# All query, key and value projections ahead of the stick-breaking attention, ten of the twelve tiles in pairs by seven block products

## Chip, cores and metric

The kernel runs on one core of a Trainium2 chip. The metric is the device time of one launch in microseconds, the median of several runs. A core has TensorE (PE: matmuls, with its weight loads shown apart as PEld), VectorE (DVE), ScalarE (ACT), GpSimd (POOL) and SyncE (SP, which only issues transfers); each works through its own instructions in order.

## What is computed

One layer of an encoder on a prompt of 1024 rows and a sample of 32 rows with a past of 512. The parts that matter here:

```python
p = h @ w_in                      # h: 1056 x 1024; columns: 384 q-latent | 256 kv-latent | 32 rope |
                                  #    512 SB q | 512 SB k | 512 SB v | 1024 gate A | 1024 gate B
def sb_attend(q, qpos, k, v, kpos):            # 8 heads of 64, strictly causal, no softmax
    z = einsum('bqhd,bshd->bhqs', q, k) * 64 ** -0.5
    sp = where(mask, softplus(z), 0.0)
    later = cumsum(sp, axis=3, reverse=True) - sp
    a = where(mask, exp(log_sigmoid(z) - later), 0.0)
    return einsum('bhqs,bshd->bqhd', a, v)
merged = sigmoid(gate A) * (o_A @ w_proj_a) + sigmoid(gate B) * (o_B @ w_proj_b)
```

`o_B` is this attention, `o_A` a latent attention with softmax that runs after it. The new keys and values are outputs too. Then come an output projection, a residual, and a convolutional feed-forward net (up-projection, down-projection). Everything is float32.

## The kernel before

**Precision.** Each operand of a product is split in a high part (rounded by ScalarE, `hi`) and a low part (the rest, by VectorE, `lo`). A product is three matmuls, high x high, high x low, low x high, added in PSUM (`mm3`, `prod`). So a *direct tile* of 128 output columns is 3 column blocks of 352 x 8 steps of the contraction x 3 = 72 matmuls (`mtile`), with the 1024 x 128 weights as the loaded operand and the transposed `h` (`Hht`, `Hlt`: 128 partitions x 8 x 1056) streaming.

**Block products.** The up-projection further down computes two such tiles together: weights and `h` are seen as 2 x 2 blocks (two halves of the contraction, two halves of the 1056 columns on the one side; the two tiles on the other), and seven products of sums of blocks take the place of eight. Each product is `prod` on column blocks of 256 and 272. Weight sums are made per pair of tiles, the sums of `h` blocks once.

**Stages, in order.** `stage_h` norms, transposes and splits `h`. `stage_sb` goes over four pairs of heads (`sb_pair`). For a pair it projects the query, key and value tile directly, splits them, turns keys and values to the row layout with TensorE transposes (`to_natural`) for the outputs and the value operand, and runs the attention of the two heads (`sb_attend`). The order of TensorE, ScalarE and VectorE within the attention is written out by hand in `ORDER`: `S` score matmuls, `a e l x c d E` the steps of the weights, `T h v` the transposed weights and their split, `V` the value product, `o p` its eviction. Among them stand `f` (three matmuls of a gate tile, or four small matmuls of a modulation product, `ada_step`), `G` (a gate block's eviction and store) and `W`/`w` (high and low part of the next gate tile's weights), which keep TensorE supplied: four of the sixteen gate tiles for each pair. The sample's rows get an attention of their own (`sb_sample`, in two halves after the second and fourth pair); its second part, `sample_rest`, runs under the next projections. `stage_lat` then makes five latent tiles directly (two kv, three q), their norms and the rotary keys, and `stage_mla` the second attention.

Outside the hand-ordered parts a planner of the tile framework orders the instructions of each engine by priority (program order) and its own cost estimates. A tile is a named buffer; a new tile of the same name and number of buffers waits until the old one is no longer read. Raw weights go through two buffers `wr`, loaded by SyncE; the splits go to two buffers each of `wh` and `wl`. Stores go through GpSimd.

Of the kernel before, what the change touches and what calls it, by code (L numbers as in the profile page):

```python
# [8 lines left out]
F32 = mybir.dt.float32  # L9
# [8 lines left out]
P = 128  # L18
# [26 lines left out]
class K:  # L45
# [9 lines left out]
    BUFS = {"A": 5, "Q": 3, "big": 3, "o": 2, "QZ": 1, "t": 5, "mh": 4, "ml": 4, "dh": 3, "dl": 3, "ada": 1, "G": 1, "Gs": 1, "xs": 1, "jk": 1, "s": 3, "pv": 1, "tr": 2, "mm": 2, "KSm": 1, "VSm": 1, "ObH": 1, "ObL": 1}  # L55
# [106 lines left out]
    def late_vectors(self):  # L162

        nc, a = self.nc, self.a
        v = self.tl(self.At, [P, TP], F32, "A")
# [109 lines left out]
    def norm_T(self, t0, xs, g, sv, tp, k0=0, k1=KT):  # L275
# [3 lines left out]
        if t0 < 8:  # L279
# [3 lines left out]
            for k in range(k0, k1, m):  # L283
                tr = self.bank("tr")
                f = self.tl(tp, [P, 512], F32, "hf").rearrange("p (k c) -> p k c", k=m)
# [15 lines left out]
        else:  # L301
# [3 lines left out]
            f = self.tl(tp, [P, 512], F32, "hf")[:, :256].rearrange("p (k t) -> p k t", t=TS)  # L305
# [98 lines left out]
    def to_natural(self, f, outs, ev):  # L404

        nc = self.nc
        for t0 in (0, 4, 8):
            tr = self.bank("tr")
            n = 4 if t0 < 8 else 1
            for j in range(n):  # L410
                r = P if t0 < 8 else TS
                nc.tensor.transpose(tr[:r, j * P : j * P + P], f[:, (t0 + j) * P : (t0 + j) * P + r], self.idt)
            ev(tr, t0, n, P if t0 < 8 else TS)

    def sb_pair(self, p):
        nc, a = self.nc, self.a
        q0, k0, v0 = 672 + p * P, 672 + 512 + p * P, 672 + 1024 + p * P

        Qe = self.tl(self.Sp, [P, TP], F32R, "Q")
        Qo = self.tl(self.Sp, [P, TP], F32R, "Q")  # L420
        wh, wl = self.w_in_tile(q0)
        for c0, n, ps in self.mtile(wh, wl, self.Hh, self.Hl, self.BLK, KT):
            m = min(n, TP - c0)
            c = slice(c0, c0 + m)
            self.hi(Qe[0:64, c], ps[0:64, :m], 0.125)
            self.hi(Qo[64:128, c], ps[64:128, :m], 0.125)
            st = nc.vector.scalar_tensor_tensor
            st(Qe[64:128, c], ps[0:64, :m], 0.125, Qe[0:64, c].bitcast(F32), ALU.mult, ALU.subtract)
            st(Qo[0:64, c], ps[64:128, :m], 0.125, Qo[64:128, c].bitcast(F32), ALU.mult, ALU.subtract)
            if m < n:  # L430
                nc.scalar.mul(self.qsb[:, p], ps[:, m:n], 0.125)
        if p == 2:
            self.sample_rest()

        KHe = self.tl(self.Sp, [P, TP], F32R, "KH")
        KHo = self.tl(self.Sp, [P, TP], F32R, "KH")
        KLe, KLo = self.KLz
        kf = self.tl(self.At, [P, BIG], F32, "big")
        wh, wl = self.w_in_tile(k0)
        for c0, n, ps in self.mtile(wh, wl, self.Hh, self.Hl, self.BLK, KT, "mm" if p else "s"):  # L440
            nc.scalar.copy(kf[:, c0 : c0 + n], ps[:, :n])
        s = slice(0, TP)
        nc.vector.tensor_copy(KHe[0:64, s], kf[0:64, s])
        nc.vector.tensor_copy(KHo[64:128, s], kf[64:128, s])
        self.lo(KLe[0:64, s], kf[0:64, s], KHe[0:64, s])
        self.lo(KLo[64:128, s], kf[64:128, s], KHo[64:128, s])
        self.hi(KHe[64:128, s], kf[0:64, s])
        self.hi(KHo[0:64, s], kf[64:128, s])
        nc.gpsimd.tensor_copy(self.ksb[:, p], kf[:, TP:T])

        def ev_out(name, after=None):
            def ev(tr, t0, n, r):
                st = self.tl(self.Sp, [P, n * P], F32, "nat" if n > 1 else "nat1")
                nc.scalar.copy(st[:r, : n * P], tr[:r, : n * P])
                pc = slice(2 * p, 2 * p + 2)
                if t0 < 8:
                    dst = a[f"sb{name}_p"][0, 0, t0 * P : (t0 + n) * P, pc].rearrange("(j r) h d -> r j (h d)", r=P)
                else:
                    dst = a[f"sb{name}_s"][0, 0, :, pc].rearrange("r h d -> r (h d)").unsqueeze(1)
                nc.gpsimd.dma_start(dst, st[:r, : n * P].rearrange("r (j c) -> r j c", j=n))  # L460
                if after:
                    after(st, tr, t0, n, r)
            return ev

        self.to_natural(kf, None, ev_out("k"))

        V = self.tl(self.Sp, [P, 8, 2, P], F32R, "V")
        vf = self.tl(self.At, [P, BIG], F32, "big")
        wh, wl = self.w_in_tile(v0)
        for c0, n, ps in self.mtile(wh, wl, self.Hh, self.Hl, self.BLK, KT):  # L470
            nc.scalar.copy(vf[:, c0 : c0 + n], ps[:, :n])

        def vsplit(st, tr, t0, n, r):
            if t0 < 8:
                sv = st.rearrange("r (j h d) -> r j h d", j=4, h=2)
                nc.vector.tensor_copy(V[:, t0 : t0 + 4, :, 0:64], sv)
                nc.vector.tensor_tensor(V[:, t0 : t0 + 4, :, 64:128], sv,
                                        V[:, t0 : t0 + 4, :, 0:64].bitcast(F32), ALU.subtract)
            else:
                nc.gpsimd.tensor_copy(self.vsb[:, p * P : p * P + P], st[:r, :P])  # L480

        self.to_natural(vf, None, ev_out("v", vsplit))

        def score(h, ps, i, c0, n):
            q = slice(i * P, (i + 1) * P)
            Q, KH, KL = (Qe, KHe, KLe) if h == 0 else (Qo, KHo, KLo)
            nc.tensor.matmul(ps[:, :n], Q[:, q], KH[:, c0 : c0 + n], start=True, stop=False)
            nc.tensor.matmul(ps[:, :n], Q[:, q], KL[:, c0 : c0 + n], start=False, stop=True)


        self.in_w.append(self.w_in_tile(2208 + 4 * p * P))
        if p == 0:
            self.late_vectors()
        E = mybir.EngineType
        with self.tc.manual_schedule(engines={E.PE, E.Activation, E.DVE}):
            self.sb_attend(score, V, self.store(self.obd[p]), self.gates(range(4 * p, 4 * p + 4)))
        if p % 2:
            self.sample_rest = self.sb_sample(p // 2)

# [24 lines left out]
        v7.0 f1 V7.1 f2 V7.0 f1 o7 f1 p7 f2 G f7 G  # L524
    """.split()

    def sb_attend(self, score, V, out, fill):
# [3 lines left out]
        common = self.sums(V, out, tiles)  # L531
        for x in self.ORDER:
            k, x = x[0], x[1:]
# [89 lines left out]
    def values(self, h, u, jb, pv, V, pt):  # L623
        for s in range(2):
            b = 2 * jb + 1 - s
            for j, x in enumerate(pt):
                self.nc.tensor.matmul(pv[:, :256], V[:, b, h], x[:, s * 256 : s * 256 + 256],
                                      start=(jb == u and s == 0 and j == 0), stop=(jb == 0 and s == 1 and j == 1))
# [1725 lines left out]
```

## Time and profile before

| | |
|---|---|
| runs | 1705.4, 1707.41, 1704.56 us; median 1705.4 |
| profiled execution | 1709.09 us; span 1707.3 us; granted clock 0.994 |
| four attention pairs, first score to last value product | 84.3 to 158.5, 200.5 to 274.0, 322.6 to 396.1, 438.0 to 511.6 us |
| latent stage | about 520 to 611 us |

The span is the time from the first to the last instruction. Busy times are shares of it; a matmul's duration overlaps the next one's, so the pace of TensorE is read from what follows it. Lnnn is a line of the kernel.

### The profile page before, as it was taken

How to read it: one execution, taken by the hardware profiler on the slowest of the kernel's cores; microseconds unless marked ns; L12 is line 12 of the kernel's file. 1: busy time of each engine (PE TensorE's matmuls, PEld its weight loads, DVE VectorE, ACT ScalarE, POOL GpSimd, SP SyncE). 2: the span in 40 equal slices, each digit the busy share in tenths (PEclk: the TensorE clock that was granted, in tenths of full speed). 3: DMA queues.
4: the chain of work that ended last, by engine and by line, in shares of the span. 5: the costliest groups of instructions: out<-in, count | busy, mean ns of one | idle time of the engine just before them, and what ended most of it. 6: DMA issues, size and time to landing. Idle time of an engine off the chain costs nothing. (4 is left out here: it accounts for less than half of the span.)

```text
span 1707.3 us, 29721 instructions
## 1 busy us (share of the span) xinstructions
PE 1674.0 (98%) x11526; PEld 1525.1 (89%) x11526; DVE 1235.1 (72%) x2065; ACT 978.2 (57%) x1902; POOL 276.6 (16%) x530
## 2 busy tenths in 40 slices
PE   5999999999999999999999999999999999999998
PEld 3899999999999898988889789999999999977886
DVE  4597495593782488787776779887787787788456
ACT  4496595593783477777773476544444444545442
POOL 2211111111110121110100121211121121110013
PEclk8999999999999999999999999999999999999999
DMA  9234343233442331222174531423333333697653
GB/s 330 82 115 126 93 125 96 87 108 86 135 130 58 98 84 55 68 76 67 63 269 148 175 125 61 143 94 130 130 100 131 131 102 131 228 328 249 227 151 121
DMA packets 169805, 224.33 MB, mean 131 GB/s; under 512 B 13326, under 2 KB 115872, under 8 KB 169664
## 3 DMA queue, kind: packets, MB, share of 16 engines
q1 hardware_dynamic: 153216, 177.11, 32.9%
q0 software_dynamic: 16224, 45.24, 7.6%
q8 instruction: 90, 1.47, 0.4%
q14 instruction: 51, 0.42, 0.1%
q10 hardware_dynamic: 224, 0.09, 0.0%
HBM read 170.34 MB, written 51.25 MB: 130 GB/s over the span
## 5 line engine op out<-in xcount | busy, mean ns | idle before, releaser
L65 ACT ACTIVATE wh<-wr 128x1024 fp32r<-128x1024 f32 (+5 forms) x153 | 130.7, 861 | 257.9 <-PE s L1808 79.6
L68 DVE TENSOR_TENSOR wl<-wr,wh 128x1024 fp32r<-128x1024 f32 (+5 forms) x153 | 150.3, 988 | 139.3 <-ACT wh L65 139.1
L72 PE MATMUL mm<-hh,wh 128*128 128x352 f32 x688 | 230.4, 335 | 0.0
L73 PE MATMUL mm<-hl,wh 128*128 128x352 f32 x688 | 224.4, 326 | 0.0
L74 PE MATMUL mm<-hh,wl 128*128 128x352 f32 x688 | 223.3, 325 | 0.0
L72 PEld LDWEIGHTS mm<-hh,wh 128*128 128x128 f32 x688 | 130.2, 189 | 7.7 <-issue 3.1
L73 PEld LDWEIGHTS mm<-hl,wh 128*128 128x128 f32 x688 | 130.2, 189 | 2.8 <-DVE hl L300 1.2
L74 PEld LDWEIGHTS mm<-hh,wl 128*128 128x128 f32 x688 | 130.0, 189 | 0.4 <-issue 0.4
L1809 PE MATMUL s<-T,wl 128*128 128x256 f32 (+1 forms) x328 | 93.6, 285 | 0.0
L1808 PE MATMUL s<-T,wh 128*128 128x256 f32 (+1 forms) x328 | 93.4, 285 | 0.0
L1807 PE MATMUL s<-T,wh 128*128 128x256 f32 (+1 forms) x328 | 93.3, 284 | 0.0
L1948 DVE SCALAR_TENSOR_TENSOR u<-u,c,u 128x1058 f32<-128x1058 f32 x68 | 87.0, 1316 | 1.9 <-ACT u L1945 0.7
L613 PE MATMUL tr<-c,A 128*128 128x128 f32 x576 | 84.5, 274 | 0.6 <-DVE A L729 0.3
L1807 PE MATMUL tr<-T,wh 128*128 128x272 f32 (+1 forms) x272 | 77.8, 286 | 0.0
L1809 PE MATMUL tr<-T,wl 128*128 128x272 f32 (+1 forms) x272 | 77.6, 285 | 0.2 <-DVE wl L68 0.2
L1808 PE MATMUL tr<-T,wh 128*128 128x272 f32 (+1 forms) x272 | 77.3, 284 | 0.0
L68 DVE TENSOR_TENSOR wl<-S,wh 128x1024 fp32r<-128x1024 f32 x40 | 48.9, 1223 | 36.8 <-ACT wh L65 36.8
L613 PEld LDWEIGHTS tr<-c,A 128*128 128x128 f32 x576 | 67.1, 141 | 7.8 <-ACT A L552 1.6
L1809 PE MATMUL mm<-T,wl 128*128 128x256 f32 (+1 forms) x256 | 73.0, 286 | 0.3 <-DVE wl L68 0.2
L1807 PE MATMUL mm<-T,wh 128*128 128x256 f32 (+1 forms) x256 | 73.0, 285 | 0.0
L1808 PE MATMUL mm<-T,wh 128*128 128x272 f32 (+1 forms) x256 | 72.7, 284 | 0.0
L68 DVE TENSOR_TENSOR PTl<-tr,PTh 128x512 fp32r<-128x512 f32 x96 | 64.5, 683 | 7.1 <-ACT PTh L65 6.8
(694 smaller groups left out, 5441.6 us busy)
## 6 DMA issues: line engine op xcount, KB each, us to landing
wr<-in_w_ada_dram SPq DMA_DIRECT2D x48, 512.0 KB, 4.5
wr<-in_w_up_dram SPq DMA_DIRECT2D x44, 512.0 KB, 3.9
dr<-in_w_down_dram SPq DMA_DIRECT2D x43, 512.0 KB, 5.0
wr<-in_w_in_dram SPq DMA_DIRECT2D x33, 512.0 KB, 4.9
wr<-gdn SPq DMA_DIRECT2D x30, 512.0 KB, 4.4
gdn<-u POOLq DMA_DIRECT2D x23, 512.0 KB, 5.4
gd<-nat POOLq DMA_DIRECT2D x48, 176.0 KB, 2.2
t<-gd SPq DMA_DIRECT2D x16, 528.0 KB, 6.1
```

Source lines behind the costliest of these rows:

```text
L65: self.nc.scalar.activation(out, in_, AF.Identity, scale=scale)
L68: return self.nc.vector.tensor_tensor(out, full, hi.bitcast(F32), ALU.subtract)
L72: m(ps, lh, rh, start=start, stop=False)
L73: m(ps, lh, rl, start=False, stop=False)
L74: self.pe = m(ps, ll, rh, start=False, stop=stop).ins
L613: self.nc.tensor.transpose(tr[:, (2 * s + q) * P : (2 * s + q + 1) * P], at[q][:, b * P : b * P + P], self.idt)
L1807: m(ps[:, :n], w[0][:, k], x[0][:, k, c], start=first and k == 0, stop=False, skip_group_check=True)
L1808: m(ps[:, :n], w[0][:, k], x[1][:, k, c], start=False, stop=False, skip_group_check=True)
L1809: i = m(ps[:, :n], w[1][:, k], x[0][:, k, c], start=False, stop=k == 3, skip_group_check=True)
L1948: nc.vector.scalar_tensor_tensor(y, u[:, w : w + YW], self.cvT[:, w, cc : cc + 1], y, ALU.mult, ALU.add)
```

## The change

All twelve query, key and value tiles are made ahead of the attention, in a new `stage_qkv`. The query and key tile of the first pair of heads are direct, and so is one q-latent tile (taken out of `stage_lat`, kept in DRAM). The other ten go in five pairs through seven block products, as in the up-projection. `stage_h` keeps the float32 `h` of the second half of the rows (`fq`), from which the sums `T1` to `T4` of `h` blocks are made while the direct tiles run. Finished high and low parts of queries and keys, and the values in row layout, are stored to DRAM (`spill`, `vd`) through GpSimd.

The attention then runs for the four pairs without projections between. The operands of a head are loaded by SyncE into single buffers: those of the next pair's first head behind the last score (`S3.1b`) and the last value product (`V3.0`) of the first head, those of the second head behind `S7.1b` and `V7.0`. The gate tiles run on through all four pairs; the first weight split of the next pair moves into the end of `ORDER`. Both halves of the sample's attention move to the latent stage, with the sample's operands kept in DRAM. The rotary table `qt` and the diagonal buffers are set up later; zeroing goes from VectorE to GpSimd.

The diff's core:

```diff
     def stage_h(self):
+        self.Fq = self.tc.alloc_tile_pool(name="fq", bufs=1, reuse_waits="tile")
+        self.fq = self.Fq.tile([P, KT, TP - 512 + TS], F32, name="fq")
...
+    def stage_qkv(self):
+        T4, T3, T1, T2 = ([Tp.tile([P, 4, HC], F32R, name=self.nm("T")) for _ in range(2)] for _ in range(4))
+        B11, B21, B22 = quad(0, 0), quad(4, 0), quad(4, 1)
+        F12, F22 = (self.fq[:, k : k + 4, 16:] for k in (0, 4))
...
+        def half(x):
+            if cnt["half"] % 2 == 0:
+                self.hs = [self.tl(self.W, [P, 1024], F32R, g) for g in ("wh", "wl")]
...
+        def sums():
+            c2 = slice(0, 264), slice(264, HC)
+            for i, q in enumerate((Q1, Q2, Q3, Q1)):
+                c, x = slice(132 * i, 132 * i + 132), q.rearrange("p (k c) -> p k c", k=4)
+                add(x, F22[:, :, c], F12[:, :, c], ALU.subtract)
+                self.hi(T3[0][:, :, c], x)
+                self.lo(T3[1][:, :, c], x, T3[0][:, :, c])
+            for c in c2:
+                x = F12[:, :, c]
+                add(x, x, fl(B11[0][:, :, c]), ALU.subtract)
+                add(x, x, fl(B11[1][:, :, c]), ALU.subtract)
+            for c in c2:
+                add(F22[:, :, c], F22[:, :, c], F12[:, :, c], ALU.subtract)
+            hi(T2, F22)
+            lo(T2, F22)
+            yield
+            hi(T1, F12)
+            lo(T1, F12)
+            yield
+            for c in c2:
+                x = F22[:, :, c]
+                add(x, fl(B21[0][:, :, c]), x, ALU.subtract)
+                add(x, x, fl(B21[1][:, :, c]), ALU.add)
+            hi(T4, F22)
+            lo(T4, F22)
+            yield
+        def pair(i, ta, tb, ua, ub):
+            ra, rb = raws.pop(0)
+            a0, a1 = half(ra[:, :512]), half(ra[:, 512:])
+            X, Y = ([self.bank(g) for _ in range(2)] for g in ("mm", "s"))
+            for ps, w, x in ((X, a0, B11), (Y, a1, B21)):
+                for b in range(2):
+                    prod(ps[b], b, w, x, True)
...
+            for b in range(2):
+                prod(X[b], b, w1, T2, False)
+                nc.scalar.copy(Q2[:, cs[b]], X[b][:, : ns[b]])
...             # then w2 x T1, w3 x T3, w4 x T4, w5 x B22 in the same way
+        pairs = ((("v", 0), ("v", 1)), (("k", 1), ("q", 1)), (("k", 2), ("k", 3)), (("v", 2), ("v", 3)), (("q", 2), ("q", 3)))
...
     ORDER = """ ...
-        v7.0 f1 V7.1 f2 V7.0 f1 o7 f1 p7 f2 G f7 G
+        v7.0 f1 V7.1 f2 V7.0 f1 o7 f1 W p7 f2 w G f7 G
...
     def stage_sb(self):
+        def queries(p, h):
+            r, o = slice(64 * h, 64 * h + 64), slice(64 - 64 * h, 128 - 64 * h)
+            d = lambda x, n: nc.sync.dma_start(x.bitcast(F32), self.spilt[n][p][r])
+            if p:
+                Q[h], KH[h] = t(f"Q{h}"), t(f"KH{h}")
+            d(Q[h][r], "qh")
+            d(KH[h][r], "kh")
+            d(KH[h][o], "kh")
+            d(Q[h][o], "ql")
+            d(self.KLz[h][r], "kl")
...
-        for p in range(4):
-            self.sb_pair(p)
+        fill = self.gates()
+        for p in range(4):
+            then = {} if p == 3 else {"S3.1b": lambda: queries(p + 1, 0), "V3.0": lambda: values(p + 1, 0),
+                                      "S7.1b": lambda: queries(p + 1, 1), "V7.0": lambda: values(p + 1, 1)}
+            with self.tc.manual_schedule(engines={E.PE, E.Activation, E.DVE}):
+                self.sb_attend(score, lambda b, h: V[h][:, b * P : b * P + P], self.store(self.obd[p]), fill, then)
...
     def stage_lat(self):
         self.sample_rest()
+        rest = self.sb_sample(0)
         fc += latent(4, 1, lp, "lt")
+        rest()
...
-        for m in range(3):
+        nc.sync.dma_start(x2, self.l2d)
+        for m in (2, 0, 1):             # m = 2 is read from DRAM, 0 and 1 are projected
```

More of the change, by code (lines that the diff above doesn't have):

```diff
@@ L445, in sb_pair @@
[L445 to L498, printed above, removed]
+            self.hi(QH[:, c], ps[:, :m], 0.125)
+            stt(QL[:, c], ps[:, :m], 0.125, fl(QH[:, c]), ALU.mult, ALU.subtract)
+            if m < n:
+                nc.scalar.mul(self.qsb[:, 0], ps[:, m:n], 0.125)
```

313 lines of the change are left out of this document (239 added, 74 removed).

## The prediction

> **What bounds the kernel now.** I read the page's first part, then the busy time by stretches (columns: us, then PE, PEld, DVE, ACT and POOL busy with their counts, granted clock, DMA share, GB/s). The stretches are the three projections between two pairs of heads (164.9 to 200.4), the attention of the first pair (84.3 to 164.9), a stretch of the later up-projection, which already makes seven block products for eight (1156.8 to 1402.5), and the latent stage (520 to 611).
>
> ```profile
> span 1707.3 us, 29721 instructions
> PE 1674.0 (98%) x11526; PEld 1525.1 (89%) x11526; DVE 1235.1 (72%) x2065; ACT 978.2 (57%) x1902; POOL 276.6 (16%) x530
> 164.90:200.40 35.50, 35.49 (x226) 34.90 (x225) 10.81 (x15) 11.28 (x22) 3.60 (x5) 1.00 0.29 80
> 84.30:164.90 80.60, 80.54 (x573) 74.93 (x572) 69.38 (x124) 65.24 (x144) 14.85 (x27) 1.00 0.41 119
> 1156.80:1402.50 245.70, 245.70 (x2049) 242.99 (x2050) 192.80 (x290) 117.08 (x189) 46.49 (x117) 1.00 0.36 119
> 520.00:611.00 91.00, 90.14 (x669) 83.77 (x667) 43.62 (x85) 39.99 (x86) 14.75 (x26) 1.00 0.31 87
> ```
>
> TensorE is never free in any of them, at full clock. Between pairs VectorE and ScalarE are busy only 10.8 and 11.3 of 35.5 us, so there the time is the matmuls' alone; in the attention they follow at 69 and 65 of 80.6 us. A saved matmul column in a projection is saved time, as long as nothing else becomes late.
>
> A busy TensorE is not a pace, because matmuls overlap. The pace comes from the evictions on ScalarE, which waits for the matmuls (ACT in order of time: start, duration; in brackets the idle time before and who ended it). First two blocks of one value tile, then the same eviction of two successive up-projection channels.
>
> ```profile
> 195.81 0.45 ACT L471 COPY big<-mm 128x352 f32<-128x352 f32 x1 [3.33 <-PE mm L74]
> 199.65 0.45 ACT L471 COPY big<-mm 128x352 f32<-128x352 f32 x1 [3.38 <-PE mm L74]
> ...
> 1158.36 0.37 ACT L1920 COPY q<-mm 128x256 f32<-128x256 f32 x1 [2.12 <-PE mm L1809]
> 1178.83 0.37 ACT L1920 COPY q<-tr 128x256 f32<-128x256 f32 x1 [0.43 <-PE tr L1809]
> ```
>
> A block is 8 x 3 = 24 matmuls of 352 columns: 3.84 us, 0.160 each. A tile of three blocks is 11.52, two tiles are 23.04 us. A channel is two tiles by seven products: 7 x 2 column blocks x 4 x 3 = 168 matmuls of 256 or 272 columns in 20.47 us, 0.122 each.
>
> **The change part by part.** *The products.* Five pairs of tiles go from 144 matmuls to 168 narrower ones, by the same helper and widths as the up-projection. 5 x (23.04 - 20.47) = **-12.9 us**. Of 17 direct tiles before (12 here, 5 in the latent stage), two query/key tiles and the latent tile stay direct in the new stage and four in the latent stage. The 72 turns of keys and values, the 16 gate tiles and the modulation products stay. So the rest of the sum is what is no longer hidden.
>
> *Does the pair of tiles keep TensorE's pace?* The work per pair, by rows that group instructions (count, busy us, mean ns of one, idle before): three on VectorE in the up-projection, then one each on VectorE, ScalarE and GpSimd between two pairs of heads.
>
> ```profile
> L68 DVE TENSOR_TENSOR wl<-S,wh 128x1024 fp32r<-128x1024 f32 x24 | 29.4, 1224 | 25.8 <-ACT wh L65 25.8
> L1899 DVE TENSOR_TENSOR S<-wr 128x512 f32<-128x512 f32 x12 | 8.3, 691 | 16.7 <-DMA wr<-in_w_up_dram 16.7
> L1884 DVE TENSOR_TENSOR u<-s,q 128x256 f32<-128x256 f32 (+1 forms) x105 | 32.5, 334 | 3.9 <-PE s L1809 2.1 <-ACT q L1920 1.8
> ...
> L428 DVE SCALAR_TENSOR_TENSOR Q<-mm,Q 64x352 fp32r<-64x352 f32 x2 | 1.0, 518 | 5.4 <-ACT Q L65 5.4
> L65 ACT ACTIVATE wh<-wr 128x1024 fp32r<-128x1024 f32 x2 | 2.1, 1060 | 6.0 <-PE mm L73 6.0
> L875 POOL DMA_DIRECT2D gd<-nat x1 | 0.5, 547 | 4.1 <-ACT nat L874 4.1
> ```
>
> Seven half splits (7 x 0.69), four weight sums (4 x 0.69), six additions of 0.33 make 9.6 us, the splits of finished tiles 2 to 5 more: at most 15 of 20.5. In the up-projection VectorE is busy 193 of 246 us, 78%, and the pace holds. I take 0.
>
> *The block sums, once.* Four operand sums over 4 x 528 = 2112 columns need six additions and four low parts: 21,120 columns. At 1224 ns for 1024 that is 25.2 us of VectorE. They can start when the last normed block is there (the last low part of the normed input on VectorE, then the first score on TensorE, as it is today):
>
> ```profile
> 61.29 0.22 DVE L68 TENSOR_TENSOR hl<-hf,hh 128x128 fp32r<-128x128 f32 x1
> 84.30 0.36 PE L487 MATMUL s<-KH,Q 128*128 128x256 f32 x1
> ```
>
> The three direct tiles now there end just before 84.3, less the value tile's turns: about 83. With the two first products, 2 x 20.47/7 = 5.8 us, the second sum is needed at 88.9, the first at 91.8, and the last (two products on) at 97.6. VectorE to the second sum: six of the ten parts, 15.1 us, plus 1.6 of query low parts (three of 0.52) and 1.2 of weight split: ready at 61.5 + 17.9 = 79.4. Then 4.2 for the pair's first weights, 1.2 for a key's low part, 2.5 for the first sum: 87.3. Then 4.3 of weights and additions, and 3.8 for the first half of the last sum: 95.4 against 97.6. It just fits if nothing waits. From 0 (it fits) to 6.5 (each low part first waits for its high part on ScalarE: 8448 columns at 1060 ns for 1024 are 8.7 us, less 2.2 of room); I take **+1.5**, near the end the count gives.
>
> *First scores.* The new stage's operand buffers become the attention's tiles. The first head's five half-height loads (256 KB each) can be issued when the third-last product is done, so two products, 5.8 us, cover them. Rows (DMA issues in the first pair's attention, KB each, us to landing; then the issue time of one on SyncE, min/median/max ns; then a stretch in which DMA was full):
>
> ```profile
> wr<-in_w_ada_dram SPq DMA_DIRECT2D x6, 512.0 KB, 4.6
> out_dram<-nat POOLq DMA_DIRECT2D x2, 256.0 KB, 3.5
> ob<-o POOLq DMA_DIRECT2D x8, 64.0 KB, 3.2
> L210 SPq DMA_DIRECT2D wr<-in_w_ada_dram x32: 327/340/1759, 69.3 to 489.8; - x32
> 20.00:40.00 20.00, 14.98 (x73) 9.86 (x67) 12.15 (x21) 13.04 (x21) 5.14 (x8) 0.59 1.04 369
> ```
>
> Five issues of 0.34 and a landing of 3.5 make 5.2 us; 1.31 MB at 369 GB/s is 3.6 us, on top of a latency of some 3. So from 0 to 11.7 (five landings one after another, 17.5 less 5.8); I take **+1.5**, by the overlapping rows. The Trainium skill, "SBUF — State Buffer", section "Door 1: The DMA port swizzle", says that 64 neighbouring partitions reach only 8 of the 16 ports. By it those loads run at half rate, 1.31 MB in 7.1 us, and this term would be about 5 us; no row here shows a 64-partition load on SyncE, and the case is a rival below.
>
> *Between pairs.* The projections between pairs also hid the attention's tail. ScalarE at the end of the first pair, the first scores after the projections (PE), and the same tail's weight split in the second pair:
>
> ```profile
> 158.54 0.36 ACT L599 COPY o<-pv 64x256 f32<-64x256 f32 x1 [2.29 <-PE pv L627]
> 164.64 0.43 ACT L874 COPY nat<-mm 128x352 f32<-128x352 f32 x1
> ...
> 200.46 0.36 PE L487 MATMUL s<-KH,Q 128*128 128x256 f32 x1
> 201.31 0.34 PE L488 MATMUL s<-KLz,Q 128*128 128x384 f32 x1
> ...
> 267.95 1.06 ACT L65 ACTIVATE wh<-wr 128x1024 fp32r<-128x1024 f32 x1 [0.93 <-DMA wr<-in_w_in_dram]
> ```
>
> The tail is filled with gate matmuls until about 163.8. Now the next pair's scores follow (0.9 us), then the modulation product, whose second weight can only be fetched into the buffer that the new `W`/`w` split frees: o7 at 158.5, high part 1.06, low part 1.22, some 161.3, plus issue and landing (0.34 + 4.6) 166.2, against 165.3 needed. That is 0.8 at each of three boundaries: **+2.4** (0 to 3 x 3). Head reloads have the whole other head's time, some 40 us (half of 80.6); they cost nothing unless SyncE holds something back (rival below). The other new transfers (16 spills of queries and keys, 8 of values, one latent tile, through GpSimd) add 25 x 0.55 us to an engine busy 3.6 of 35.5; I take 0.
>
> *Latent stage.* It loses one tile (11.5 us) of cover and gains the first half of the sample's attention, whose matmuls come along from the projections of the third pair. Today's stalls there:
>
> ```profile
> 296.05 0.66 PE L785 MATMUL pv<-A,big 128*128 128x64 f32 x4 [0.33 <-ACT A L772]
> 553.82 0.63 PE L1030 MATMUL tr<-c,nat 128*128 128x128 f32 x4 [0.82 <-DMA nat<-in_cache_mla_krope_dram]
> ```
>
> Two stalls of 0.3 and 0.8 us. The sample's first half gets the second latent tile as its new cover, VectorE and ScalarE are half idle (44 and 40 of 91). From -0.3 to +4; I take **+1.0**, net of the first stall **+0.7**. The rotary table, loaded later, has the key and value products before its first use: 0.
>
> Sum: -12.9 + 1.5 + 1.5 + 2.4 + 0.7 = **-6.8 us**. The profiled execution took 1709.1 us, its span 1707.3; the median of the runs is 1705.4. Taken off each: 1702.3 for the profiled execution, **1698.6** for the median.
>
> **The rivals.**
> *All cover holds* (products gain in full, every other term at its lower end): -12.9 - 0.3 = -13.2, 1692.2. For it: the up-projection's pace without a stall. Chance 0.25.
>
> *The first pair and the first scores come late*: sums at some 6 us and half-rate loads at 5 instead of 1.5 each: -6.8 + 8 = +1.2, 1706.6. For it: VectorE just fits, ScalarE and VectorE hand the sums to each other, and 64 KB from 64 partitions took 3.2 us where 256 KB from 128 took 3.5. Against: the loads use both halves in turn. Chance 0.14.
>
> *SyncE's one queue starves the gates* (the slower case). The head reloads wait on SyncE for the last score of the old head, and the weight loads of the gate tiles stand behind them. Today SyncE waits long for buffers (waits by who released: us in total, times, longest):
>
> ```profile
> SPq L82 <- PE mm L212: 150.8, 16, 13.6
> ```
>
> and the tail's split above waited 0.93 us for its weights, so these have no slack. ScalarE and TensorE run in a written order and would stop behind the late split. At 2.5 us for each of six places (two heads, three boundaries) it is +15: -6.8 + 15 = +8.2, 1713.6. It turns the result from 1.1 us a place. Against: the loads are placed just after those scores, where little else is due. Chance 0.13.
>
> *It does not do what it says*: if a matmul cost its weight load and not its columns, 24 more a pair at 0.160 would add 3.84 instead of taking 2.57: +19.2 - 6.8 + 12.9 = +25, 1731. The row against it: the weight loads are busy 98 to 99% in both stretches, yet the pace follows the columns (0.160 for 352, 0.122 for 264 on average). The Trainium skill, "Perfetto Trace Analysis", section "Identifying the Most-Contended Engine", judges TensorE's headroom by that busy share; the trace shows the share equal and the pace different, so I leave it 0.02.
>
> **How the numbers follow.** The forecast has 0.46. What a measurement of this kernel can tell from no change is 0.2%, 3.4 us. Faster: the forecast, full cover and a part of the late case (0.03): 0.74. Same: most of the late case: 0.11. Slower: SyncE's queue and weight loads: 0.15. The range 1691.0 to 1706.6 holds forecast, full cover and late case: 0.85, and their edges leave some 0.8.
>
> **What would show it.** Right: 120 more matmuls; the five pairs at 20.5 us each; the first scores at 83 + 5 x 20.47 and the turns of keys and values, 186 to 196 us; pair periods of 80 to 82 us instead of 116; the latent stage shorter by a tile. Wrong: gaps on TensorE released by VectorE's sums, by loads of queries or keys, or by ScalarE waiting for gate weights at the boundaries; a pace over 0.125 us in the block products; attention periods well over 82 us.

## The result, and the profile after

The changed kernel is slower: 1729.5 us (1728.6 to 1731.7) against 1705.0 us for the kernel before on the same chip, a ratio of 1.0143 (95%: 1.0126 to 1.0161). The forecast was 1698.6, the range 1691.0 to 1706.6. The profiled execution took 1731.7 us.

Page, first part, and busy time by stretches of the changed kernel (us, then PE, PEld, DVE, ACT, POOL busy with counts, granted clock, DMA share, GB/s): two steady stretches of the seven products, then the first block pair (80 to 110), then the first scores (200 to 230).

```profile
span 1729.9 us, 30270 instructions
PE 1669.2 (96%) x11646; PEld 1518.2 (88%) x11646; DVE 1273.2 (74%) x2129; ACT 992.7 (57%) x1934; POOL 294.6 (17%) x566
160.00:180.00 20.00, 20.00 (x169) 19.98 (x168) 8.74 (x14) 9.66 (x19) 4.71 (x8) 1.00 0.56 172
180.00:200.00 20.00, 20.00 (x169) 19.96 (x168) 11.66 (x21) 8.18 (x20) 5.30 (x9) 1.00 0.48 151
80.00:90.00 10.00, 8.36 (x66) 7.91 (x64) 5.90 (x7) 3.68 (x8) 3.17 (x5) 1.00 0.47 162
90.00:100.00 10.00, 2.82 (x10) 2.33 (x11) 10.00 (x12) 6.01 (x7) 0.00 (x0) 0.52 0.00 0
100.00:110.00 10.00, 9.94 (x66) 9.66 (x66) 7.89 (x12) 2.91 (x6) 0.00 (x0) 0.79 0.42 105
200.00:210.00 10.00, 8.54 (x71) 8.30 (x69) 5.45 (x11) 3.48 (x8) 5.46 (x11) 1.00 1.08 308
210.00:220.00 10.00, 1.54 (x13) 0.81 (x13) 2.72 (x3) 2.11 (x2) 3.84 (x8) 0.67 1.04 361
220.00:230.00 10.00, 5.78 (x23) 4.51 (x23) 1.81 (x5) 2.98 (x9) 0.19 (x1) 0.65 0.85 317
```

There are 120 more matmuls and 5 us less TensorE time (1669.2 against 1674.0). In the steady stretches 169 matmuls take 20 us, one more than a pair's 168 in the forecast 20.5. The loss stands in two places of some 20 us each, where TensorE is nearly empty.

I added up, over the trace, each matmul's distance to the next one beyond its pace in a steady stretch (0.160 us for 352 columns, 0.122 for 264, and so on). From 30 us to the first score of the later, latent attention this idle time is 33.2 us more than before, the work at pace is 13.2 us less: 20.0 us longer in all. The rest of the kernel adds 2.5 us at its end, which no run here explains.

**First place: the first block pair.** TensorE in order of time (idle time before, and who ended it); then VectorE; then ScalarE.

```profile
95.42 0.58 PE L2003 MATMUL s<-T,wh 128*128 128x256 f32 x1 [7.06 <-ACT wh L65]
97.99 0.58 PE L2003 MATMUL mm<-T,wh 128*128 128x256 f32 x1 [1.76 <-ACT wh L65]
```

```profile
71.25 0.69 DVE L68 TENSOR_TENSOR wl<-wr,wh 128x512 fp32r<-128x512 f32 x1 [0.18 <-ACT wh L65]
82.35 1.23 DVE L68 TENSOR_TENSOR S<-S,sg 128x1024 fp32r<-128x1024 f32 x1 [10.41 <-PE tr L456]
85.33 1.33 DVE L538 TENSOR_TENSOR q<-fq 128x528 f32<-128x528 f32 x2 [1.75 <-DMA l2d<-q]
86.57 1.25 DVE L543 TENSOR_TENSOR fq<-fq,hh 128x1056 f32<-128x1056 f32 x1
```

```profile
81.41 0.45 ACT L642 COPY q<-pv 128x352 f32<-128x352 f32 x1 [3.40 <-PE pv L74]
```

TensorE waits 7 us for weights and operand sums. But VectorE, which makes the sums, is idle for 10.4 us just before. Two of the four chunks of the third operand sum (`q<-fq`, L538) ran at 57.7 and 59.9; the other two start only at 85.3, released by the store `l2d<-q`. They go through `Q2` and `Q3`, and these are slices of `Q0`, the tile that takes the latent tile's eviction (`lf`, last block at 81.4) until it is stored. The in-place sums (L543) must stand behind those chunks, so everything waits.

**Second place: the first scores.** TensorE, then ScalarE, then SyncE's issues.

```profile
210.58 0.39 PE L1099 MATMUL s<-KL,Q 128*128 128x256 f32 x1 [2.04 <-POOL KL L1084]
220.94 1.08 PE L211 MATMUL mm<-wr,cT 128*32 128x256 f32 x8 [8.82 <-DMA wr<-in_w_ada_dram]
230.31 0.66 PE L1098 MATMUL s<-KH,Q 128*128 128x512 f32 x1 [3.59 <-DVE A L726]
```

```profile
214.21 1.06 ACT L65 ACTIVATE sg<-fq 128x1024 fp32r<-128x1024 f32 x1 [7.44 <-issue]
217.05 1.06 ACT L65 ACTIVATE sg<-fq 128x1024 fp32r<-128x1024 f32 x1 [1.78 <-DMA sbd<-sb]
226.79 0.55 ACT L708 ACTIVATE A<-s 128x128 f32<-128x128 f32 x2 [8.68 <-DMA ql<-fq]
```

```profile
206.72 0.60 SPq L1094 DMA_DIRECT2D V<-vd  x1
207.51 6.39 SPq L207 DMA_DIRECT2D ada<-in_b_ada_dram  x4
214.00 0.36 SPq L209 DMA_DIRECT2D wr<-in_w_ada_dram  x1
```

GpSimd's issues of the last two value stores:

```profile
204.74 0.54 POOL L475 DMA_DIRECT2D vd<-sg  x1 [3.36 <-DVE sg L474]
206.99 0.54 POOL L475 DMA_DIRECT2D vd<-sg  x1 [0.43 <-DVE sg L474]
```

The first score comes at 208.3, the fourth score block (`S1.1`) at 230.3: 22.1 us, against 4.7 before (200.5 to 205.1). Three waits overlap. The zeroing of the low key tiles stands behind stores on GpSimd. The second modulation weight stands in SyncE's queue behind the loads of both heads and the bias, whose four small issues alone took 6.4 us. And ScalarE's first activation waits for the store of a low query part: the new score tile `A` begins 14,720 bytes into a place whose first 17,408 bytes are `fq`, from which that store reads. The store is also issued late: ScalarE splits the last two query tiles (`sg<-fq`) only at 214.2 and 217.1, and the stage buffers `sg` that it writes are those that the last value stores read (issued at 204.7 and 207.0, landing a median of 9.3 us later; that these ended the idle 7.4 us is read from the times, since the profile names no releaser). The transfers themselves are slow here (DMA issues between 190 and 230 us, KB each, median us to landing):

```profile
DMA packets 7570, 12.03 MB, mean 301 GB/s; under 512 B 592, under 2 KB 5312, under 8 KB 7568
...
vd<-sg POOLq DMA_DIRECT2D x4, 512.0 KB, 9.3
...
KH<-kh SPq DMA_DIRECT2D x4, 256.0 KB, 8.1
```

Before the change the same 40 us moved 5.5 MB.

### The profile page after: what moved, and what is told of

Its sections match the earlier page's. It is cut to its first block, busy times and chain, and to the rows that moved or that the text cites. A ratio compares the mean times of both kernels' runs of the same rounds, so it can differ in the third digit from the quotient of the medians.

```text
span 1729.9 us, 30270 instructions
## 1 busy us (share of the span) xinstructions
PE 1669.2 (96%) x11646; PEld 1518.2 (88%) x11646; DVE 1273.2 (74%) x2129; ACT 992.7 (57%) x1934; POOL 294.6 (17%) x566
## 5 line engine op out<-in xcount | busy, mean ns | idle before, releaser
L72 PE MATMUL mm<-hh,wh 128*128 128x352 f32 x456 | 155.3, 341 | 0.0
L73 PE MATMUL mm<-hl,wh 128*128 128x352 f32 x456 | 150.5, 330 | 0.2 <-DVE hl L302 0.2
L74 PE MATMUL mm<-hh,wl 128*128 128x352 f32 x456 | 149.6, 328 | 0.0
L2003 PE MATMUL mm<-T,wh 128*128 128x256 f32 (+1 forms) x376 | 109.5, 292 | 1.8 <-ACT wh L65 1.8
L2004 PE MATMUL mm<-T,wh 128*128 128x256 f32 (+1 forms) x376 | 108.3, 288 | 0.0
L68 DVE TENSOR_TENSOR wl<-S,wh 128x1024 fp32r<-128x1024 f32 (+1 forms) x55 | 59.0, 1077 | 48.9 <-ACT wh L65 48.5
L72 PEld LDWEIGHTS mm<-hh,wh 128*128 128x128 f32 x456 | 87.4, 192 | 7.2 <-ACT o L755 3.3
L73 PEld LDWEIGHTS mm<-hl,wh 128*128 128x128 f32 x456 | 87.4, 192 | 3.2 <-DVE hl L302 1.7
L74 PEld LDWEIGHTS mm<-hh,wl 128*128 128x128 f32 x456 | 87.4, 192 | 0.4 <-issue 0.3
L65 ACT ACTIVATE wh<-S 128x1024 fp32r<-128x1024 f32 (+1 forms) x55 | 51.6, 942 | 48.7 <-PE s L2004 13.1
L2003 PEld LDWEIGHTS mm<-T,wh 128*128 128x128 f32 x376 | 72.0, 191 | 3.9 <-ACT wh L65 3.3
```

The source lines that it names most:

```text
L65: self.nc.scalar.activation(out, in_, AF.Identity, scale=scale)
L68: return self.nc.vector.tensor_tensor(out, full, hi.bitcast(F32), ALU.subtract)
L72: m(ps, lh, rh, start=start, stop=False)
L73: m(ps, lh, rl, start=False, stop=False)
L74: self.pe = m(ps, ll, rh, start=False, stop=stop).ins
L2003: m(ps[:, :n], w[0][:, k], x[0][:, k, c], start=first and k == 0, stop=False, skip_group_check=True)
```

## The experiments

The theory after the first look: the products bring what was forecast, and two stalls, each from places and queues that are shared, take more than that back. The rivals: VectorE has no capacity for the operand sums; the transfers themselves, 12 MB in 40 us, are the limit, wherever buffers lie.

The table puts the kernels together. They ran on several chips, on which the kernel before took 1705.0 to 1707.5 us, so medians from different chips can differ by 2.5 us for that alone; the ratios are to the kernel before on the same chip. "Pair 1" is TensorE's idle time beyond its pace from 80 to 110 us; "S1.1" is the time from the first score block to the fourth, in us; "gap" the longest distance of two matmuls between 80 and 240 us.

| kernel | median us | ratio to before (95%) | pair 1 | first score at | S1.1 | gap |
|---|---|---|---|---|---|---|
| changed | 1729.5 | 1.0143 (1.0126 to 1.0161) | 13.5 | 208.3 | 22.1 | 9.2 |
| e1_sums | 1723.4 | 1.0097 (1.0079 to 1.0115) | 5.9 | 198.4 | 21.4 | 12.2 |
| e2_late | 1732.4 | 1.0152 (1.0137 to 1.0167) | 13.5 | 208.2 | 20.9 | 9.7 |
| e3_nat | 1726.5 | 1.0116 (1.0100 to 1.0131) | 13.4 | 206.5 | 19.3 | 10.6 |
| e4_start | 1719.4 | 1.0082 (1.0065 to 1.0099) | 12.2 | 205.2 | 13.1 | 7.4 |
| e5_all | 1714.0 | 1.0042 (1.0027 to 1.0057) | 6.1 | 200.7 | 11.0 | 3.0 |
| e6_turn | 1712.0 | 1.0035 (1.0022 to 1.0048) | 6.2 | 200.1 | 11.3 | 3.6 |
| e7_direct | 1725.1 | 1.0111 (1.0095 to 1.0126) | 1.0 | 210.9 | 12.7 | 8.5 |
| e8_place | 1718.5 | 1.0072 (1.0058 to 1.0086) | 0.9 | 199.6 | 21.4 | 10.0 |
| e9_place | 1712.6 | 1.0037 (1.0025 to 1.0050) | 1.2 | 192.0 | 20.5 | 9.3 |
| e10_ada | 1708.5 | 1.0016 (1.0007 to 1.0025) | 1.2 | 192.4 | 17.9 | 8.3 |
| e11_start | 1710.9 | 1.0029 (1.0019 to 1.0038) | 1.2 | 192.7 | 19.2 | 11.3 |
| e12_start | 1701.7 | 0.9974 (0.9964 to 0.9984) | 0.9 | 190.8 | 8.7 | 3.4 |

**e1_sums: the third operand sum through one buffer.**

```diff
-            for i, q in enumerate((Q1, Q2, Q3, Q1)):
+            for i, q in enumerate((Q1, Q1, Q1, Q1)):
```

> The third operand sum takes all four of its chunks through the one buffer Q1 instead of Q1, Q2, Q3, Q1, so no chunk shares a buffer with the latent tile's eviction any more. Theory (shared buffer): the sums run while the latent tile is still multiplied, the gap of 7.2 us on TensorE at 88.1 us and the 2.1 us one behind it go, the first pair takes 21 to 24 us, and the time falls by 10 to 13 us from 1729.5 to 1716.5 to 1719.5. Rival (VectorE's capacity: the twenty-five microseconds of sums do not fit before 89 us): a gap of 5 us or more stays at the second sum, and the time stays above 1724.

The long gap is gone and the first score comes 9.9 us earlier. VectorE had the capacity all along (e1_sums, VectorE: three of the four chunks with the first in-place sum among them, then the first pair's weight sum):

```profile
55.84 0.70 DVE L538 TENSOR_TENSOR q<-fq 128x528 f32<-128x528 f32 x1
58.01 0.71 DVE L538 TENSOR_TENSOR q<-fq 128x528 f32<-128x528 f32 x1
58.75 1.26 DVE L543 TENSOR_TENSOR fq<-fq,hh 128x1056 f32<-128x1056 f32 x1
...
63.24 0.70 DVE L538 TENSOR_TENSOR q<-fq 128x528 f32<-128x528 f32 x1
...
88.60 0.69 DVE L575 TENSOR_TENSOR S<-wr 128x512 f32<-128x512 f32 x1 [1.53 <-DMA kl<-S]
```

The first two chunks run about when they did, the third at 63.2 instead of 85.3, and the in-place sums (L543) begin at 58.8 instead of 86.6. What is left, a gap of 2.7 us at 87.3, is a second shared place: the weight sum goes into `S1`, which is also the first key's tile, and waits for the store of its low part (`kl<-S`). The time fell by 6.1 us (7.8 by the ratios), less than the 10 to 13 expected; S1.1 still takes 21.4 us, and the wait for the modulation weight grew from 9.1 to 12.1.

**e2_late, e3_nat, e4_start: the start of the attention.** First SyncE's order alone, then the place alone, then both with the zeroing moved.

```diff
-        for h in range(2):
-            queries(0, h)                       # and V[h]
+        load(0)                                 # head 0; head 1: then["S2.1a"] of the first pair
...
-        for g, w, n in (("o", 256, 2), ("big", BIG, 3)):
+        for g, w, n in (("o", 256, 2), ("big", BIG, 3), ("nat", 512, 2)):
...
-            nc.gpsimd.memset(self.KLz[h][64 - 64 * h : 128 - 64 * h].bitcast(F32), 0.0)
+            nc.vector.memset(self.KLz[h][64 - 64 * h : 128 - 64 * h].bitcast(F32), 0.0)
```

> Only head 0 of the first pair is loaded up front; the six loads of head 1 are issued from the first pair's own order, after its score S2.1a, so that in SyncE's queue the modulation's bias and weight stand ahead of them. Theory (SyncE's order makes the modulation weight late): TensorE's gap of 9.1 us at 211.7 falls under 3 us; but ScalarE's first activation still waits for the store of the last low query part (it started at 226.8), so the time falls by 2 to 7 us only. Rival (the bytes: DMA is full there, and order does not matter): the weight lands within 2 us of where it did (220.9), and the time stays within 2 us of 1729.5.

> Two more buffers are placed at the start of the attention's pool, so that its score tiles no longer lie where the projections' result tiles lay, from which the low query parts are still being stored. Theory (shared place): ScalarE's first activation starts right behind the first score, near 211 to 213 instead of 226.8; TensorE's 9.1 us wait for the modulation weight stays, the 3.9 us one behind it goes; 4 to 9 us less than 1729.5. Rival (the bytes): the first activation waits elsewhere, and the time stays within 2 us of 1729.5.

> The two edits to the start of the attention together (head 1 loaded from the pair's order, score tiles placed apart from the result tiles), and the zeroing of the low key tiles on VectorE instead of behind the stores on GpSimd. Theory (three waits, of which each alone hides the others): from the first score to S1.1 some 5 to 8 us instead of 22.1 (4.7 before the change), and 14 to 18 us less than 1729.5: 1711.5 to 1715.5. Rival (the bytes bound this stretch: 12.0 MB between 190 and 230 us at the 335 GB/s seen are 36 us): under 6 us less. The stall in the first block pair stays in any case.

With the order alone (e2) the weight lands at 214.0 instead of some 221, and its gap falls to 3.2 us. The time does not fall, where 2 to 7 us less were expected (its interval overlaps with the changed kernel's): ScalarE's first activation still starts only at 225.6, and TensorE waits 9.6 us a little later. With the place alone (e3) the activation starts at 216.9, ten us earlier, and the 3.9 us gap goes, but not the one for the weight (10.5 us); 3.0 us were gained, 4 to 9 expected. Together, with the zeroing moved as well, they bring 10.1 us, and S1.1 falls by 9.0. So the waits do hide each other; what the zeroing gives was not run by itself. The size was missed: 14 to 18 us less and S1.1 at 5 to 8 were expected. Against the rival of the bytes stands that the same 12.0 MB (185 to 225 us) now delay less.

**e5_all, e6_turn: all edits together, and the weight split at the end of `ORDER`.**

```diff
-        v7.0 f1 V7.1 f2 V7.0 f1 o7 f1 W p7 f2 w G f7 G
+        v7.0 W f1 V7.1 f2 V7.0 w f1 o7 f1 p7 f2 G f7 G
```

> The chunks of the third operand sum through one buffer, and the three edits to the start of the attention, together. Theory (two separate stalls, each with its own causes): the gains add, 9.9 us of earlier first scores (208.3 to 198.4 in the kernel with the first edit alone) on top of the 9 us of the other three (22.1 to 13.1 us from the first score to S1.1): 1708 to 1712. Rival (a stall that ends early only meets the DMA queues fuller, as the wait for the modulation weight grew from 9.1 to 12.1 us when the first stall went): the gains eat each other, 1714 or more.

> As the kernel with all four edits, and at the end of the attention's written order the split of the next gate weight (W and w) stands 1.5 us further ahead, before the last two value products instead of behind the last output. Theory (the weight buffer frees late): the gaps of 0.8 to 1.1 us at the three boundaries between pairs go, 2 to 3 us less than the kernel with the four edits. Rival (the landing of the modulation weight is late for the transfers, not for its buffer): gaps and time stay.

e5 took 1714.0 us, outside the 1708 to 1712 of the theory and on the border of the rival. In sum the gains do nearly add: 6.1 + 10.1 = 16.2 alone, 15.5 together (by the ratios 18.2 and 17.2). In e6 no gap over 0.5 us is left at a boundary, and the periods fall from 78.6 and 79.0 to 78.0 and 78.3 us. The medians differ by 2.1 us, as expected, though the intervals of the two overlap.

**e7_direct: what the seven products bring.** The five pairs computed as ten direct tiles, without operand sums, in the same stage.

```diff
-            # seven products per pair
+            for x, u in zip(raws.pop(0), (ua, ub)):
+                wh, wl = self.wsplit(x)
+                for c0, n, ps in self.mtile(v(wh), v(wl), self.Hh, self.Hl, self.BLK, KT, "mm s"):
+                    nc.scalar.copy(u[:, c0 : c0 + n], ps[:, :n])
+                    bg(2)
```

> As the kernel with all four edits, but the ten tiles of the five pairs are each computed directly, 72 matmuls of 352 columns a tile, without operand sums, and still ahead of the attention, stored to DRAM and loaded again. It parts what the seven products bring from what the detour costs. Theory (the products bring the forecast 12.9 us, and the sums cost 1 to 3): 10 to 13 us more than the kernel with the four edits, and no stall in the first pair at all. Rival (the seven products bring less in this stage than their pace says, since sums and evictions slow them): less than 5 us more. Either way the difference to the kernel before is then the price of the detour itself.

11.1 us more than e5, within the 10 to 13 expected, and pair 1 has almost no idle time. The difference is not the products alone: e5 still has the 5 us wait for `S1` in pair 1 that e7 lacks, and e7 starts its attention 1.7 us slower. In work at pace up to the latent attention e7 does some 13.9 us more. In e7 the detour through DRAM costs 1725.1 less 1707.5 (before, on the same chip) = 17.6 us, more than seven products can bring; much of it is the start of the attention again (S1.1 at 12.7).

**e8_place to e12_start: what the remaining stall is.** These edits take away, one after another, what the last trace shows ScalarE or TensorE waiting for.

```diff
 # e8: first key's low part in its own buffer; late vectors loaded a pair ahead; head 0 zeroed on GpSimd
+                low = low if p else sg()
 # e8, e9: places of the score tiles (e8: on fq again; e9: from 27,008 bytes on)
-        for g, w, n in (("o", 256, 2), ("big", BIG, 3)):
+        for g, w, n in (("big", BIG, 2), ("A", TP, 3), ...                                     # e8
+        for g, w, n in (("o", 256, 1), ("nat", 512, 2), ("PTh", 512, 2), ("PTl", 512, 2), ...   # e9
 # e10: in the first gate tile
-                yield from self.ada_step(2, self.W, self.Sp, ada)   # ahead of its matmuls
+                        if m == b == 0 and k == 4:
+                            yield from ad                           # behind five steps of them
 # e11: e3's places; next raw weight asked for behind the second modulation weight; and
-                QH = sg()
+                QH = sg() if p < 2 else U[p][:, :TP].bitcast(F32R)
 # e12: the sample's tile sb first in its pool, the score tiles behind it; head 1 behind S3.1a
+        self.sample_views(A.tile([P, 768], F32, name="sb"))               # ahead of S1
-        for g, w, n in (("o", 256, 2), ("big", BIG, 3), ("nat", 512, 2)):
+        for g, w, n in (("o", 256, 2), ("big", BIG, 3), ("nat", 512, 2), ("pad", 416, 1)):
-                then["S2.1a"] = lambda: load(1)
+                then["S3.1a"] = lambda: load(1)
```

> As the kernel with the moved weight split, and four more edits against what its trace still shows waiting: the first key's low part goes to a buffer of its own instead of the one that the weight sums of the first pair use (they waited until 90.3 us for its store); the late vectors' loads are issued a pair ahead of their turns (TensorE waited 1.3 us at 136.6); the zeros of head 0's low key on GpSimd and head 1's on VectorE (the second score matmul waited 3.5 us at 200.1); and the attention's tiles are placed so that the first score tiles lie on result tiles long stored (ScalarE waited 1.9 us at 206). Theory (what is left of the two stalls is shared buffers and queue order): the first pair falls to 21 to 22 us, S1.1 comes 5 to 6 us behind the first score, and 7 to 11 us go from 1712.0: 1701 to 1705, by 0.2 to 0.4% under the kernel before. Rival (the transfers themselves: DMA is full from 200 to 230 us): the first scores still take 10 us or more, and the time stays at 1707 or above.

> As the kernel with the placed tiles, with the placing mended: the first score tile lies on the sum buffer S1, the next on Q1 and Q0, and the places of the tile that still holds the low query parts go to buffers used later; the late vectors' turns stand a pair behind their loads. Theory (the first activation, at 217.5 us there, waited because its tile shared its place with that stored tile): it starts by 207 us, S1.1 comes 8 to 12 us behind the first score instead of 22, the 2.2 us at the late vectors go; 1705 to 1709, 10 to 13 us less than with the first placing. Rival (what is late is the transfers, wherever the tiles lie): under 5 us less.

> As the kernel with the mended placing, and in the first gate tile the two modulation products stand behind five matmul groups of the gate instead of ahead of them. Theory (the modulation weight lands some 5 us after TensorE asks for it, and nothing else is asked for): the gap of 4.9 us falls under 2.5, less 0.8 for an eviction that now comes late; 1 to 3 us less than the kernel with the mended placing, 1703 to 1706, no slower than the kernel before. Rival (TensorE then only waits for the next score, whose tiles the activations hold): no difference over 1 us.

> As the kernel with the modulation products moved, with three changes at the first scores: the high parts of the last two query tiles go to the places of the last two value tiles instead of the two stage buffers that the value stores still hold; the attention's tiles are placed as in the kernel with two more placed buffers (the first waits left there, 209 us for the second score tile, were for those stage buffers); and in the first gate tile the next raw weight is asked for behind the second modulation weight, whose buffer came free only at 199.8 us. Theory (each of these waits is a shared buffer): the first activation starts by 196 us, S1.1 comes 10 to 13 us behind the first score instead of 18, no gap on TensorE is over 4 us, and the time falls by 4 to 8 us from 1708.5: 1700 to 1704, at last under the kernel before. Rival (DMA is full from 190 to 210 us, and something there is late wherever buffers lie): a gap of 6 us or more stays, and under 3 us are gained.

> As the kernel before it, with head 1's six loads (1.8 MB) asked for behind the score S3.1a, where SyncE first waits for the next raw weight's buffer, and the projections' small sample tile at the front of its pool, so that no score tile shares a place with it (its store, 9.9 us long, held the second score tile until 208.3 us). Theory (the transfers themselves: DMA is full from 190 to 210 us, and every store and load there takes 7 to 12 us to land; taking 1.8 MB away shortens all the others): no transfer in that stretch takes over 8 us, the largest gap on TensorE falls from 11.2 to under 5 us, and 4 to 8 us go from 1710.9: 1703 to 1707, level with the kernel before or under it. Rival (the clock, 0.5 to 0.6 while TensorE idles, and other buffers keep it): under 3 us.

ScalarE's first activations of the score tiles, one fence each for e8, e9, e11 and e12, and behind them GpSimd's issue of the sample tile's second store in e12:

```profile
217.45 0.55 ACT L724 ACTIVATE A<-s 128x128 f32<-128x128 f32 x2 [11.74 <-DMA ql<-fq]
```

```profile
197.93 0.26 ACT L724 ACTIVATE A<-s 128x128 f32<-128x128 f32 x1
209.16 0.38 ACT L724 ACTIVATE A<-s 128x256 f32<-128x256 f32 x1 [10.97 <-DMA qh<-sg]
```

```profile
195.28 0.26 ACT L724 ACTIVATE A<-s 128x128 f32<-128x128 f32 x1
208.45 0.38 ACT L724 ACTIVATE A<-s 128x256 f32<-128x256 f32 x1 [12.90 <-DMA sbd<-sb]
```

```profile
193.66 0.26 ACT L724 ACTIVATE A<-s 128x128 f32<-128x128 f32 x1
196.15 0.38 ACT L724 ACTIVATE A<-s 128x256 f32<-128x256 f32 x1 [2.23 <-issue]
```

```profile
196.79 0.55 POOL L668 DMA_DIRECT2D sbd<-sb  x1
```

e8 settles the first pair: with the second shared place gone, 0.9 us of TensorE's idle time is left from 80 to 110. The operand sums cost nothing. But my placing was wrong: the first score tile lay on `fq` again, on a part long read. The wait is for the tile's last reader, not for the bytes' own. So the start was slower than in e6, and the time rose by 6.5 us, where 7 to 11 less were expected. e9 mends that for the first tile. The buffers of one name lie together, so the tiles did not come to lie quite as its expectation says: the first is on `Q1` and `Q0`, and the second waits for the store of a stage buffer. The expected 12 us at most to S1.1 were missed by far (20.5), the time fell by 5.9 of the 10 to 13 expected. In e10 the modulation products moved back, but with them the weight buffer that the second one needs: it was asked for only at 199.8, TensorE waited 8.2 us where under 2.5 were expected. 4.2 us were gained all the same (1 to 3 expected), so not for the reason given: the second score tile was free at 207.0 instead of 209.2. e11 mends both, and now the second score tile waits for the small sample tile's store. The time rose by 2.4 us, with overlapping intervals, where 4 to 8 less were expected. Here the rival seemed right: something is late wherever buffers lie.

e12 speaks against it. No distance of two matmuls over 3.4 us is left, S1.1 comes 8.7 us behind the first score, and 1701.7 us are 9.2 less than e11 and 0.26% under the kernel before. Its expectation was met for the gap, and the time fell further than the 4 to 8 us expected, but not for the reason given. DMA is as full as ever (busy time by stretches, then DMA issues between 185 and 225 us):

```profile
190.00:200.00 10.00, 6.34 (x46) 4.81 (x46) 7.53 (x15) 4.91 (x13) 6.96 (x10) 0.91 1.06 371
200.00:210.00 10.00, 10.00 (x50) 9.61 (x49) 6.18 (x12) 6.73 (x16) 1.11 (x2) 0.75 1.05 325
```

```profile
V<-vd SPq DMA_DIRECT2D x2, 512.0 KB, 9.5
...
ql<-fq POOLq DMA_DIRECT2D x2, 512.0 KB, 8.2
...
sbd<-sb POOLq DMA_DIRECT2D x1, 128.0 KB, 10.1
```

The store that kept ScalarE from e11's score tile for 12.9 us takes 10.1 us here, against 9.8 there; only nothing lies where it reads. ScalarE writes the second score tile at 196.2, before the second of the sample tile's two stores is even issued (196.8), so this wait is gone by the place of the tile and not by faster transfers. SyncE asked for head 1's last five loads only 1 to 2 us later than in e11. The two edits were not run apart, so how much of the 9.2 us the later loads add is open. The bytes may still cost something: S1.1 is 4.0 us later behind the first score than in the kernel before.

## Why the prediction was wrong, point by point

**The products** (-12.9): right. The work at pace fell by 13.2 us. That e7 against e5 gives 11.1 us, beside a forecast of 11.4 for products less sums, is partly luck, since e5 still holds the wait for `S1`.

**Pace of a pair** (0): right. 169 matmuls in 20 us with VectorE at 9 to 12 of 20 us.

**The block sums** (+1.5, 0 to 6.5): wrong; pair 1 lost some 12.5 us (13.5 less the 0.9 to 1.2 of e8 to e12). The step that failed is "VectorE to the second sum: ready at 79.4". It counted VectorE's work and asked when its inputs are there, not when its output buffers are free. Two buffers were not: `Q0` (7.6 us, e1) and `S1` (some 5 us, e1 to e8). Both stood in the whole diff, as `kf, lf = S0, Q0`. The count itself was good: with free buffers (e8 to e12, against e7) the term is 0 to 0.3, the lower end.

**First scores** (+1.5, 0 to 11.7): wrong; S1.1 came 17.4 us later behind the first score than before. The step that failed is "I take +1.5, by the overlapping rows". It counted five loads for one head, with the landing times of a quiet stretch (3.5 us). It left out what else is in the same queues: the stores of the last pairs (landing in 6 to 9 us), the other head's loads, the modulation weight and bias behind them on SyncE, the zeroing behind the stores on GpSimd, the last query split behind the stage buffers of the value stores, and the places that the score tiles take over. With most of these waits taken away (e12) S1.1 is 4.0 us later than before, inside the range, and the first score, forecast for 186 to 196 us, comes at 190.8 instead of 208.3. Loads at half rate, weighed there as a reason for 5 us, are not told apart by any run: between later pairs (330 to 380 us) the quarter-megabyte loads of 64 partitions land in 3.7 to 6.1 us, half-megabyte loads of 128 in 5.0 to 6.1. That is no reason for 17 us.

**Between pairs** (+2.4): right. Three gaps, as forecast (waits of TensorE from 300 to 640 us: total, times, longest):

```profile
PE mm L211 <- DMA wr<-in_w_ada_dram: 2.0, 3, 0.8
```

The periods are 78.8 and 78.9 us, a little under the forecast 80 to 82.

**Latent stage** (+0.7): right within its bounds; from the last value product to the first latent score 93.3 us instead of 99.1, with gaps of 0.5 and 0.7.

**The rivals.** The late first pair and first scores was the right place at a third of the price: 1.5 + 1.5 became 6 + 5 there, and 12.5 + 17.4 on the chip. The rival of SyncE's one queue named one of the three mechanisms, head loads ahead of a weight that TensorE needs; it did not happen at the six places named but at the one start that I had priced by loads alone. *It does not do what it says*, priced at 1731, comes nearest to the measured 1729.5, by luck: its mechanism, a matmul that costs its weight load, is not there, since 169 matmuls take 20 us. By place and sum: -13.2 (work at pace) + 12.5 + 18.9 (idle time from the first to the seventh score block, 20.4 less 1.5) + 2 (boundaries) = +20.2, against the 20.0 of the trace up to the latent attention; smaller differences elsewhere cancel.

The range failed because the two unknown terms were bounded by counts of instructions and transfers alone, and because no bound took in the time that TensorE then runs slower. Behind the two gaps the granted clock is 0.52 and 0.79, and 0.67 and 0.65. In pair 1 the two gaps themselves are 9.3 of the 13.5 us; the other 4 are matmuls that follow one another more slowly, with a clock of 0.50 from 90.5 to 104.1 although no gap over 1 us follows 98.0. The Trainium skill, "TensorE: Matmul & The Clock Gate", section "What's actually happening", says that the clock falls to half after an idle window of some 3.4 us and comes back after as long under load. The trace agrees in kind; in e12 0.75 was granted from 200 to 210 behind a gap of 3.4 us. A shorter gap cost clock as well: behind e1's 2.7 us at 87.3, 0.51 was granted from 91.4 to 94.8.

## What to carry to other kernels

When a change moves work ahead of a stage, list for each buffer of the new work who had the place last and when that one's store lands; a place is free when its last reader is done, and for a reader that is a DMA in a full stretch this was 7 to 12 us after the issue, not 3.5. Price the start of a new stage by everything in its queues, stores and zeroing too, not by the loads it needs. An idle engine just before a stall (VectorE 10.4 us here) suggests that the stall is no question of capacity: look for the buffer. And fix such waits together: of the edits to the start, the order alone brought nothing (e2) and the place alone 3.0 us (e3), since the next wait stood right behind it; with the zeroing added the two brought 10.1 (e4).

## What was not expected of the hardware

A small transfer need not be faster than a large one where DMA is full: the 128 KB store of the sample tile took 10.1 us in e12, half-megabyte stores beside it 6.9 to 8.2 (a 64 KB one 5.7), and the four bias loads of 32 KB took SyncE 6.4 us to issue in the changed kernel. The Trainium skill, "DMA: Bandwidth & Descriptors", section "Issuing engines are not separate DMA queues", says that transfers of all issuing engines share the same 16 engines; the DMA share of 1.04 to 1.08 in these stretches, with GpSimd's stores and SyncE's loads late together, agrees.
